# Token-major out projections: 128-token blocks stand still, 512 weight columns move, norms run along the rows

## The chip, the cores and the metric

One core of one Trainium2 chip. The time is device microseconds of one execution of the whole program; a kernel's time is the median of its runs. A profiled execution leaves a trace with every instruction's start, length and what it waited for. Engines are named as in the profile: PE is TensorE's matmuls, PEld its weight loads, DVE is VectorE, ACT ScalarE, POOL GpSimd, SP SyncE, which here issues the DMAs.

## What is computed

One inference step of a trunk with two layers over 640 tokens of 2048 features: 128 context tokens (condition c_ctx) and 512 sample tokens (condition c). In each layer

```
shift, scale, gate = split(silu(cond) @ w_ada + b_ada)
h = rmsnorm(x) * norm_w * (1 + scale) + shift
p = h @ w_in                                   # split among the layer's mixers
x = x + gate * (concat(mixers(p)) @ w_out)     # the out projection, 2048 x 2048
```

The even layer's mixers are a gated DeltaNet and a windowed attention, the odd layer's a gated linear attention and a neighbourhood attention. At the end y = rmsnorm(x) * final_norm_w. The change is in the last line of each layer, in the norm that follows it, and in how x gets from there to layer 1 and to y. Gates differ between the two groups of tokens, not between tokens of a group.

## The kernel before

**Layout.** Activations are feature-major: a slice k of 128 features lies on the partitions, the 640 tokens along the row. Each product is kept near float32 by splitting both factors into a high and a low part of type float32r: three matmuls, high by high, high by low, low by high (`G.mm`, line 77 of the profile, is the call that issues every matmul; `G.tr`, line 84, a transpose).

**Weights.** `weights()` (L1041) brings 256 KB from memory into `w_st` (SyncE's queue, L1046), ScalarE casts it to `w_hi` (L1049) and VectorE subtracts to get `w_lo` (L1051; GpSimd for a few). There are three buffers of each. `Main.load` keeps three such loads ahead of the matmuls, and `Main.step` runs one small group of three matmuls at a time; whoever needs a result calls `until`, which steps until it is there and, every so many steps, advances a side job, the "fill".

**Out projection** (`Outs`, `out_proj` L1503). 16 blocks of 128 output features; the weight block is the stationary operand (128 x 128), 320 tokens move, in two halves, into two accumulators of 128 x 320. The 16 slices of the mixers' output, in an order in which they become ready (ORDER0, ORDER1), are loaded from a buffer in memory and split into `hh` and `hl` by `Outs.stream`. Fourteen blocks are done whole; the last two are done first for tokens 0 to 319, then for 320 to 639, so that the norm of the first half can start early. After a block `residual` loads `x_old` (L1515), computes gate * acc + x_old on VectorE (L1519), writes layer 0's x to memory (L1523), squares it on ScalarE (L1462), sums the squares over blocks on GpSimd (L1463) and multiplies x by the next norm's weight (`scaled`, L1423).

**Norm.** `rstd` sums the squares over the partitions with small matmuls against ones (`n_ss`), takes the root on VectorE (lines 96 to 101), and spreads it to all partitions with another matmul (`n_bc`) and a copy to `n_R`. `times` (L1427) multiplies.

**After the projections.** Layer 0's `end` scales x into `h_t`, adds the shift on ScalarE (`hh`, L1773) and subtracts on VectorE (`hl`, L1774), for each half, and layer 1's first matmuls (`turns`, half by half) start on the first half. Layer 1's `end` scales x and writes yT (L1856).

**The fill of layer 0's projection** is `ada_vec` (L1295): layer 1's shift, computed on VectorE from w_ada, 256 KB a step (`vec`, L1306 the loads, L1318 and L1320 the products), four parts that each end with a few small matmuls (`adv_ps`). It advances once in six groups of three matmuls. From the last two blocks on the order of instructions is pinned to the order of the program (`g.pin`).

Of the kernel before, what the change touches and what calls it, by code (L numbers as in the profile page):

```python
# [18 lines left out]
EPS = 1e-6  # L19
T = 640  # L20
# [43 lines left out]
SMALL = [("bada", 96), ("nw", 32), ("fn", 16), ("convw", 120), ("dtb", 16), ("alog", 16), ("sink", 8), ("onorm_a", 1),  # L64
# [1002 lines left out]
class Main:  # L1067


    def __init__(self, g, hh, hl, part={}, start=0):  # L1070
        self.part, self.start = dict(part), start
        self.g, self.hh, self.hl, self.order = g, dict(enumerate(hh)), dict(enumerate(hl)), range(16)
        self.asked, self.quarters, self.loaded, self.cur, self.n = [], [], [], None, 0
        self.done, self.ready, self.other, self.last = 0, {}, [], []
# [28 lines left out]
    def halves(self, drams):  # L1103

        rs = [[[d, 0, None, False, None, (t,)] for d in drams] for t in range(2)]
        self.last = [(r, q) for t in rs for r in t for q in range(4)]
        return [[self.wait(r, True) for r in t] for t in rs]

    def load(self):
        while len(self.loaded) < LOOK:  # L1110
# [9 lines left out]
            if r[0].shape[1] == 512:  # L1120
# [4 lines left out]
            self.loaded.append((q, work))  # L1125
# [40 lines left out]

    def when(self):
# [6 lines left out]
        q = self.loaded[0][0]  # L1174
        return max(self.ready.get(k, 0 if k in self.hh else INF) for k in self.order[q * 4:q * 4 + 4])
# [72 lines left out]
def ada(g, l, parts, m, store, wait=None):  # L1248
# [26 lines left out]
    for i, (c, d, k0, k1) in enumerate(todo):  # L1275
# [13 lines left out]
        if k1 == 16:  # L1289
            yield LAT["hop"]  # L1290
            ada_out(g, l, parts, c, acc)
            yield


def ada_vec(g, l, part, store, engs, wait=None):  # L1295
# [14 lines left out]
    for i, (c0, k) in enumerate(todo):  # L1310
# [27 lines left out]
        ada_out(g, l, (part,), c0, rows)  # L1338

# [126 lines left out]
class Outs:  # L1466


    def __init__(self, g, main, total, w, order, halves=0):
        self.g, self.main, self.total, self.w, self.order, self.whole = g, main, total, w, order, 16 - halves  # L1470
# [16 lines left out]
    def stream(self):  # L1487
# [4 lines left out]
        self.reqs = [m.ask(self.w[n], n, True) for n in range(self.whole)]  # L1492
        self.halves = m.halves([self.w[n] for n in range(self.whole, 16)])
# [9 lines left out]
def out_proj(g, l, outs, pool, x_old, x_spill, fill, scale, end=None):  # L1503
# [4 lines left out]
    accs, xs, todo, xos = [], [], [], {}  # L1508
    main, reqs = outs.main, outs.reqs
    gate = g.mod[l, 2]  # L1510

    def residual(n, ps):
        if n not in xos:
            xos[n] = g.pt2.tile([128, T], F32, name="x_old", bufs=4)
            nc.sync.dma_start(xos[n], x_old(n))  # L1515
            xs.append(pool.tile([128, T], F32, name=f"x{n}"))
        for t in ps:
            for c0, c1, cd in ((0, 128, 0), (128, 320, 1)) if t == 0 else ((320, 640, 1),):
                nc.vector.scalar_tensor_tensor(out=xs[n][:, c0:c1], in0=ps[t][:, c0 - t * 320:c1 - t * 320],  # L1519
                                               scalar=gate[:, n, cd:cd + 1], in1=xos[n][:, c0:c1], op0=ALU.mult, op1=ALU.add)  # L1520
        cs = slice(min(ps) * 320, max(ps) * 320 + 320)
        if x_spill is not None:
            nc.sync.dma_start(x_spill(n)[:, cs], xs[n][:, cs])  # L1523
        square_sum(g, pool, accs, xs[n], n, nc.gpsimd, cs=cs)
        todo.append((n, cs))
        while todo and scale(todo[0][0]) is not None:
            i, cs = todo.pop(0)
            scaled(g, xs[i], scale(i), cs)

    for n in range(outs.whole):  # L1530
        ps = main.until(reqs[n], fill, 6)
        if n == 15:
            for _ in fill:
                pass
        residual(n, ps)
    g.pin = True
    for t in range(2 if outs.whole < 16 else 0):
        for n in range(outs.whole, 16):
            residual(n, main.until(outs.halves[t][n - outs.whole], fill, 3))
        for _ in fill:  # L1540
            pass
        fill = end(t, xs, accs)
    for _ in fill:
        pass
    return xs, accs


def body(nc, tc, I, O):
    off = [(k, v.shape[1]) for k, v in const_table().items()]
    with ExitStack() as es:  # L1550
        g = G()
        g.nc, g.tc, g.I, g.O = nc, tc, I, O
        g.mod, g.mods = {}, {}
# [25 lines left out]
        g.fn, g.dtb, g.alog, g.sink = (cuts[k] for k in ("fn", "dtb", "alog", "sink"))  # L1579
# [68 lines left out]
        x1 = g.pd1.tile([16, 128, T], F32, name="x1_d")  # L1648


        with ExitStack() as e1:
# [98 lines left out]
            outs = g.outs = Outs(g, main, 53, I["w_out_even"], ORDER0, 2)  # L1750
# [235 lines left out]
```

## Time and profile before

| | before |
|---|---|
| median of 3 runs | 2717.81 us (2716.46 to 2723.16) |
| the profiled execution, its span | 2723.34 us, 2721.5 us |
| mean granted TensorE clock | 0.983 |
| matmuls of one out projection, weight loads | 1536 of 128x320, 72 of 256 KB |
| matmuls between 2698 and 2722 us | 17 |

How to read the profile's rows: a timeline row has the start and length in us, the engine, the line, the operation, the tiles written and read, the shapes, and in brackets the engine's idle time before it and what ended it. "128*128 128x320 f32" is a stationary operand of 128 columns and an output of 128 x 320. A group row has a count, the busy time and the mean length in ns; a mean mixes what the group mixes. In a table of stretches, each engine has its busy time and, in brackets, its number of instructions; the clock is the one granted to TensorE, and the DMA share can come out above 1. Matmuls overlap, so their price is the distance of starts and not the length. SPq rows are DMA issues, with the time that the queue took for the issue and not for the transfer.

### The profile page before, as it was taken

The page shows a single profiled execution, that of the slowest core. Times are in us where ns is not written, and L with a number is a line of the kernel's source. Part 1 is how long each engine was busy: PE and PEld are TensorE (multiplying, and loading weights), DVE is VectorE, ACT ScalarE, POOL GpSimd, SP SyncE. Part 2 cuts the span into 40 slices and gives each one's busy share as a digit, 9 for nine tenths or more (in the row PEclk, how much of TensorE's full clock was granted, in tenths as well). Part 3 has the DMA queues.
Part 4 walks back from the last instruction along what each step waited for, and adds up shares of the span by engine and source line. Part 5 has one row for each costly group of instructions (what it writes and reads, how often), then busy time and mean ns, then how long its engine had stood idle before and what let it go on. Part 6 is the DMA issues. An engine that isn't in the chain of part 4 may idle for free.

```text
span 2721.5 us, 54637 instructions
## 1 busy us (share of the span) xinstructions
PE 2601.2 (96%) x21303; PEld 2435.2 (89%) x21303; DVE 1536.9 (56%) x3598; ACT 954.0 (35%) x2150; POOL 704.9 (26%) x894
## 2 busy tenths in 40 slices
PE   6989999999999999999999899999999999999996
PEld 4779788988978997799998899999999999998996
DVE  5766546656556565357876755546453644545225
ACT  3232343433433343442224443343333434233222
POOL 2326514253251550001223330012001301221113
PEclk9989999999999999999999999999999999999998
DMA  9932434243243424246653413323232222325324
GB/s 334 309 97 71 116 95 122 81 133 116 85 126 111 123 60 136 72 143 200 214 186 115 127 64 105 106 76 97 81 108 90 87 93 87 98 69 183 99 97 136
DMA packets 264706, 329.85 MB, mean 121 GB/s; under 512 B 76013, under 2 KB 148925, under 8 KB 264447
## 3 DMA queue, kind: packets, MB, share of 16 engines
q1 hardware_dynamic: 264447, 326.35, 38.2%
q8 instruction: 168, 2.75, 0.4%
q14 instruction: 91, 0.75, 0.1%
HBM read 294.95 MB, written 28.68 MB: 119 GB/s over the span
## 4 chain that ended last, share of the span: by engine, by line
PE 44%; DVE 3%; DMA 2%; issue 1%; ACT 0%; DVEq 0%; SPq 0%; ACTq 0%
PE acc L77 38%; PE at_s L77 1%; PE at_o L77 1%; DMA vec<-w_ada 1%; PE c_lv L77 1%; DVE hl L1774 1%; DVE vec L1320 1%; PE c_ops L77 1%; PE tm_ps L84 1%; PE c_U L77 0%; DVE x L1427 0%; PE at_pt L84 0%; DVE w_lo L1051 0%; PE c_bp L77 0%; DMA hl<-o_d 0%
## 5 line engine op out<-in xcount | busy, mean ns | idle before, releaser
L77 PE MATMUL acc<-hh,w_hi 128*128 128x320 f32 (+1 forms) x4544 | 1446.7, 319 | 18.7 <-ACT w_hi L1049 5.7
L77 PE MATMUL acc<-hl,w_hi 128*128 128x320 f32 (+1 forms) x4544 | 1415.6, 312 | 7.7 <-DVE hl L1229 7.7
L77 PE MATMUL acc<-hh,w_lo 128*128 128x320 f32 x4480 | 1394.4, 311 | 4.8 <-DVE w_lo L1051 4.8
L77 PEld LDWEIGHTS acc<-hh,w_hi 128*128 128x128 f32 (+1 forms) x4544 | 856.5, 189 | 59.8 <-issue 32.8
L77 PEld LDWEIGHTS acc<-hl,w_hi 128*128 128x128 f32 (+1 forms) x4544 | 857.5, 189 | 12.9 <-DVE hl L1229 11.0
L77 PEld LDWEIGHTS acc<-hh,w_lo 128*128 128x128 f32 x4480 | 847.3, 189 | 7.4 <-DVE w_lo L1051 6.7
L1051 DVE TENSOR_TENSOR w_lo<-w_st,w_hi 128x512 fp32r<-128x512 f32 x561 | 439.1, 784 | 588.1 <-ACT w_hi L1049 578.5
L1049 ACT CAST w_hi<-w_st 128x512 fp32r<-128x512 f32 (+1 forms) x604 | 365.2, 605 | 925.1 <-PE acc L77 783.9
L1320 DVE SCALAR_TENSOR_TENSOR vec<-vec,cond 128x256 f32<-128x256 f32 (+1 forms) x360 | 212.3, 634 | 23.3 <-DMA vec<-w_ada 21.5
L496 POOL TENSOR_TENSOR i_S<-i_S,i_tmp 40x30 f32<-40x30 f32 (+14 forms) x240 | 141.1, 588 | 18.7
L494 POOL TENSOR_TENSOR i_tmp<-i_S 40x30 f32<-40x30 f32 (+14 forms) x240 | 134.2, 559 | 18.0
L1463 POOL TENSOR_TENSOR n_acc<-n_acc,n_sq 128x640 f32<-128x640 f32 (+1 forms) x30 | 45.9, 1530 | 298.2 <-ACT n_sq L1462 298.2
L77 PE MATMUL ada_ps<-adv,cond 128*32 128x128 f32 x2048 | 94.7, 293 | 25.4 <-DMA adv<-w_ada 24.9
L929 POOL TENSOR_TENSOR c_X<-c_b 128x320 f32<-128x320 f32 x56 | 46.1, 822 | 221.9 <-PE c_lv L77 195.0
L77 PEld LDWEIGHTS ada_ps<-adv,cond 128*32 128x32 f32 x2048 | 48.7, 113 | 53.5 <-DVE n_acc L1463 19.4
L215 DVE SCALAR_TENSOR_TENSOR a_y<-a_pad,consts,a_y 128x644 f32<-128x644 f32 x96 | 89.7, 934 | 2.2
L790 POOL TENSOR_TENSOR d_bias<-d_braw,d_mask 128x256 f32<-128x256 f32 x32 | 27.9, 905 | 231.8 <-PE tm_ps L84 90.7
L1287 DVE TENSOR_TENSOR adv<-adv,ada_ps 128x128 f32<-128x128 f32 x144 | 40.5, 281 | 73.3 <-PE ada_ps L77 72.4
L301 POOL TENSOR_TENSOR a_at<-a_df,consts 128x640 f32<-128x640 f32 x8 | 13.7, 1712 | 253.9 <-DVE a_ss L269 222.0
L665 POOL TENSOR_TENSOR b_sw<-b_sw,b_tab 128x512 f32<-128x512 f32 x10 | 14.9, 1491 | 234.8 <-DMA b_sw<-b_q 199.7
L404 ACT ACTIVATE a_ot<-a_st,g_egc 128x128 f32<-128x128 f32 x72 | 26.4, 367 | 107.2 <-PE a_st L77 105.7
L1051 POOL TENSOR_TENSOR w_lo<-w_st,w_hi 128x256 fp32r<-128x256 f32 (+1 forms) x43 | 36.3, 851 | 106.6 <-ACT w_hi L1049 89.0
(310 smaller groups left out, 2760.6 us busy)
## 6 DMA issues: line engine op xcount, KB each, us to landing
adv<-w_ada SPq DMA_DIRECT2D x256, 256.0 KB
w_st<-w_in_odd SPq DMA_DIRECT2D x232, 256.0 KB
w_st<-w_in_even SPq DMA_DIRECT2D x188, 256.0 KB
w_st<-w_out_even SPq DMA_DIRECT2D x72, 256.0 KB
w_st<-w_out_odd SPq DMA_DIRECT2D x72, 256.0 KB
vec<-w_ada SPq DMA_DIRECT2D x64, 256.0 KB
vec<-w_ada SPq DMA_DIRECT2D x128, 128.0 KB
hl<-o_d SPq DMA_DIRECT2D x31, 320.0 KB
```

The lines of the kernel that those rows point to most:

```text
L77: i = self.nc.tensor.matmul(out, lhsT=lhsT, rhs=rhs, **kw)
L84: i = self.nc.tensor.transpose(out, x, ident)
L215: nc.vector.scalar_tensor_tensor(out=y, in0=pad[:, j:j + CL], scalar=w[:, j:j + 1], in1=y, op0=ALU.mult, op1=ALU.add)
L494: E.tensor_tensor(out=t, in0=S[:, j + 1:, j].unsqueeze(2).to_broadcast([40, n, j]), in1=S[:, j, 0:j].unsqueeze(1).to_broadcast([40, n, j]) ...
L496: E.tensor_tensor(out=S[:, j + 1:, 0:j], in0=S[:, j + 1:, 0:j], in1=t, op=ALU.add)
L790: nc.gpsimd.tensor_tensor(out=bias[:, j], in0=braw[:, :, x0:x0 + 32], in1=g.dmask[:, j * 32:j * 32 + 32].unsqueeze(1).to_broadcast([128, 8 ...
L929: nc.gpsimd.tensor_tensor(out=pv(X[0])[:, :, 1 - d], in0=bv[:, :, 1 - d], in1=bm, op=ALU.subtract)
L1049: nc.scalar.copy(hi, st)
L1051: (nc.gpsimd if g.spare >= 0 else nc.vector).tensor_tensor(out=lo, in0=st, in1=hi, op=ALU.subtract)
L1287: nc.vector.tensor_add(acc, acc, ps)
L1320: nc.vector.scalar_tensor_tensor(out=acc[:, c], in0=st, scalar=sc, in1=acc[:, c], op0=ALU.mult, op1=ALU.add)
L1463: eng.tensor_add(accs[0][:, cs], accs[0][:, cs], t[:, cs])
```

## The change

Both out projections are turned round. Their order of loops, the layout of x, the norms and the output change with that; the mixers and the input projections don't.

- **Matmuls.** The stationary operand is a 128 x 128 piece of the mixers' output: slice k, tokens of block b. The moving one is 512 columns of w_out, slice k, laid out so that one load of 256 KB holds one slice (`by_512`; before, a load held four slices of 128 columns). Accumulators are 128 tokens x 512 features, in two pools of three (`pacc`, `pax`); the general pool `psg` goes from four to two. There are four column blocks n and five token blocks b. For n = 0 and n = 3 the tokens go in two groups, (0, 1, 2) and (3, 4), for n = 1 and 2 all five at once: 6 passes over 16 slices, 96 loads a projection, 960 matmuls of 512 columns.
- **Residual.** The gate now varies along the row: `gate_rows` transposes it, stores it to memory once, and `out_proj` loads it spread over all partitions for each n (128 x 2 x 512). VectorE multiplies the accumulator by it into `g_t`, GpSimd adds that to x (VectorE for n = 3), ScalarE squares with a running sum along the row (`n_ss`). x is loaded token-major from a new input and, in layer 1, from the spilled copy; the loads of the next n are asked for when an n begins. Layer 1 multiplies by the final norm's weight, a new input spread over the partitions (1 MB in the tile), on GpSimd for n < 3.
- **Norm.** `token_rstd` sums four numbers per token and takes the root on VectorE; no matmuls.
- **Layer 0's end.** Each token block is scaled by a number per partition (blocks shared out to ScalarE, VectorE and GpSimd), then 80 transposes bring x back to feature-major, ScalarE applies scale and shift, VectorE casts `hh`, GpSimd subtracts `hl`. The first group's stand among the matmuls of the last pass.
- **Layer 1's end.** y is scaled and written token-major, 256 KB a store.
- **The fill** advances once in three groups.

The diff, cut to its core (the first `end` is layer 0's, the second layer 1's):

```diff
+    def wide(self, drams):
+        parts = [(0, 1, 2), (3, 4)]
+        rs = []
+        for n, d in enumerate(drams):
+            for bl in parts if n in (0, len(drams) - 1) else [(0, 1, 2, 3, 4)]:
+                rs.append([d, 0, {}, set(), None, bl, n])
...
+    def tokens(self, r, i, w):
...
+        for b in r[5]:
...
+            cs = slice(b * 128, b * 128 + 128)
+            for x, wt, e in ((self.hh, hi, 0), (self.hh, lo, 1), (self.hl, hi, 2)):
+                g.mm(r[2][b], lhsT=x[k][:, cs], rhs=wt, start=i == 0 and e == 0, stop=i == 15 and e == 2)
...
-def out_proj(g, l, outs, pool, x_old, x_spill, fill, scale, end=None):
+def out_proj(g, l, outs, pool, x_old, x_spill, fill, every, end, fn=None):
...
+    def load(n):
+        if n < 4:
+            cs = slice(n * 512, n * 512 + 512)
+            gates[n] = g.pt2.tile([128, 2, 512], F32, name="gate", bufs=2)
+            nc.sync.dma_start(gates[n], g.gate[l][:, cs].unsqueeze(0).to_broadcast([128, 2, 512]))
+            for b in range(5):
+                nc.sync.dma_start(xs[b][:, cs], x_old(b)[:, cs])
...
+        for b in bl:
+            ps = main.until(main.block(r, b), fill, every)
+            x = xs[b][:, cs]
+            t = g.pt2.tile([128, 512], F32, name="g_t", bufs=2)
+            nc.vector.tensor_tensor(out=t, in0=ps, in1=gates[n][:, int(b > 0)], op=ALU.mult)
+            (nc.vector if n == 3 else nc.gpsimd).tensor_tensor(out=x, in0=x, in1=t, op=ALU.add)
+            if x_spill is not None:
+                nc.sync.dma_start(x_spill(b)[:, cs], x)
+            junk = g.pt2.tile([128, 512], F32, name="n_sq")
+            nc.scalar.activation(junk, x, AF.Square, accum_out=ss[:, b, n:n + 1])
+            if fn is not None and n < 3:
+                nc.gpsimd.tensor_tensor(out=x, in0=x, in1=fn[:, cs], op=ALU.mult)
...
+            def end(bl, xs, ss):
+                yield
+                r = token_rstd(g, px, ss, bl)
...
+                for k in range(16):
+                    ps = g.psg.tile([128, 3, 128], F32, name="h_ps", tag="gen")
+                    for j, b in enumerate(bl):
...
+                        g.tr(ps[:, j], x, g.c["ident"])
...
+            def end(bl, xs, ss):
+                r = token_rstd(g, px, ss, bl)
...
+                for n in (3, 0, 1, 2):
...
+                        nc.sync.dma_start(O["y"][b][:, cs], x)
```

SyncE's queue where layer 1's projection begins, before (`hl` is the last slice of the mixers' output, `x_old` a block of x, `w_st` the weights):

```order
L1499 DMA hl_28634<-o_d 128x640
L1515 DMA x_old<-x_d 128x640
L1046 DMA w_st<-w_out_odd 128x512
L1515 DMA x_old<-x_d 128x640 x3
L1046 DMA w_st<-w_out_odd 128x512
```

and after (`fn` the final norm's weight, `x_28291` to `x_28295` the five token blocks):

```order
L1536 DMA hl_28251<-o_d 128x640
L1931 DMA fn<-fn 128x2048
L1585 DMA gate<-gate_d_28189 128x2x512
L1587 DMA x_28291<-x_d 128x512
...
L1587 DMA x_28295<-x_d 128x512
L1585 DMA gate<-gate_d_28189 128x2x512
L1587 DMA x_28291<-x_d 128x512
...
L1587 DMA x_28295<-x_d 128x512
L1046 DMA w_st<-w_out_odd 128x512 x3
```

Seven slices of weights have been asked for by then; the eighth to tenth (k7 to k9) now follow fn, two gates and ten x, where one x_old stood before. The same queue where layer 0's projection begins, before:

```order
L1046 DMA w_st<-w_out_even 128x512
L1306 DMA vec<-w_ada 128x512 x4
L814 DMA d_mask<-d_tab 128x256
L781 DMA d_v<-cn_v 128x128
L1046 DMA w_st<-w_out_even 128x512
```

and after:

```order
L1046 DMA w_st<-w_out_even 128x512
L1587 DMA x_15320<-x 128x512
...
L1587 DMA x_15324<-x 128x512
L1341 DMA vec<-w_ada 128x512 x4
L1046 DMA w_st<-w_out_even 128x512 x3
L1587 DMA x_15320<-x 128x512
```

Ten loads of x now stand with the four of vec ahead of the seventh slice (k6), and behind the three slices k6 to k8 come ten more with three of vec. VectorE in the first blocks of layer 0's projection, before (`vec` is the fill):

```order
L1320 SCALAR_TENSOR_TENSOR vec<-vec,cond 128x512 x4
L1051 TENSOR_TENSOR w_lo<-w_st,w_hi 128x512
L1320 SCALAR_TENSOR_TENSOR vec<-vec,cond 128x512 x4
L1051 TENSOR_TENSOR w_lo<-w_st,w_hi 128x512
L1320 SCALAR_TENSOR_TENSOR vec<-vec,cond 128x512
```

and after, in the second group of n = 0:

```order
L1355 SCALAR_TENSOR_TENSOR vec<-vec,cond 128x512 x2
L1051 TENSOR_TENSOR w_lo<-w_st,w_hi 128x512
L1355 SCALAR_TENSOR_TENSOR vec<-vec,cond 128x512
L1051 TENSOR_TENSOR w_lo<-w_st,w_hi 128x512
L1355 SCALAR_TENSOR_TENSOR vec<-vec,cond 128x512 x2
L1051 TENSOR_TENSOR w_lo<-w_st,w_hi 128x512
```

A weight difference now stands behind one or two steps of the fill instead of four.

More of the change, by code (lines that the diff above doesn't have):

```diff
@@ L1101, in turns, with block @@
         return [both(r) for r in rs]
[L1103 to L1107, printed above, removed]
+    def wide(self, drams):
[4 more added lines that the diff above has]
+                rs.append([d, 0, {}, set(), None, bl, n])
+        self.last = [(r, i) for r in rs for i in range(16)]
+        return rs
+    def block(self, r, b):
+        while b not in r[3]:
+            yield lambda: b in r[3]
+        return r[2][b]
     def load(self):
@@ L1119, in load @@
             r, q = self.quarters.pop(0)
[L1120 removed]
+            ks = range(q * 4, q * 4 + 4)
+            if r[0].shape[1] == 8192:
+                work = self.tokens(r, q, weights(self.g, r[0], q * 4, q * 4 + 4))
+                ks = [q]
+            elif r[0].shape[1] == 512:
                 work = self.narrow(r, q, narrow(self.g, r[0], q))
@@ L1338, in ada_vec @@
         ada_out(g, l, (part,), c0, rows)
+        if part == 2 and c0 + width == 2048:
+            yield 5
+            gate_rows(g, l)
 def ada_put(g, l, part, n0, ps):
@@ L1500, in stream, with gate_rows @@
                 self.take(k, x, lo)
-def out_proj(g, l, outs, pool, x_old, x_spill, fill, scale, end=None):
+def gate_rows(g, l):
+    nc = g.nc
+    m = g.mod[l, 2]
+    ps = g.psg.tile([16, 2, 128], F32, name="gr_ps", tag="gen")
+    for c in range(2):
+        g.tr(ps[:, c], m[:, :, c], g.c["ident"])
+    rows = g.pk.tile([16, 2, 128], F32, name="gr", tag="gr")
+    nc.scalar.copy(rows, ps)
+    g.gate[l] = g.pd1.tile([2, 2048], F32, name=f"gate_d{l}")
+    nc.sync.dma_start(g.gate[l].rearrange("c (n p) -> n c p", p=128), rows)
@@ L1506, in out_proj @@
+def out_proj(g, l, outs, pool, x_old, x_spill, fill, every, end, fn=None):
     fill = iter(fill)
     nc = g.nc
[L1508 to L1528, printed above, removed]
@@ L1530, in out_proj @@
-    for n in range(outs.whole):
-        ps = main.until(reqs[n], fill, 6)
-        if n == 15:
+    main = outs.main
+    xs = [pool.tile([128, 2048], F32, name=f"x{b}") for b in range(5)]
+    ss = pool.tile([128, 5, 4], F32, name="n_ss")
+    gates = {}
+    def load(n):
[5 more added lines that the diff above has]
+                nc.sync.dma_start(xs[b][:, cs], x_old(b)[:, cs])
@@ L1533, in out_proj @@
             for _ in fill:
                 pass
[L1535 to L1542, printed above, removed]
+            fill, every = end(bl, xs, ss), 1
     for _ in fill:
         pass
-    return xs, accs
 def body(nc, tc, I, O):
@@ L1552, in body @@
         g.nc, g.tc, g.I, g.O = nc, tc, I, O
-        g.mod, g.mods = {}, {}
+        g.mod, g.mods, g.gate = {}, {}, {}
+        g.pax = None
         g.spare = 0
```

145 lines of the change are left out of this document (96 added, 49 removed).

## The prediction

> **What bounds the kernel now.** I read the page first: the span, the engines' busy shares and the chain that ended last.
>
> ```profile
> span 2721.5 us, 54637 instructions
> PE 2601.2 (96%) x21303; PEld 2435.2 (89%) x21303; DVE 1536.9 (56%) x3598; ACT 954.0 (35%) x2150; POOL 704.9 (26%) x894
> ...
> PE acc L77 38%; PE at_s L77 1%; PE at_o L77 1%; DMA vec<-w_ada 1%; PE c_lv L77 1%; DVE hl L1774 1%; DVE vec L1320 1%; PE c_ops L77 1%; PE tm_ps L84 1%; PE c_U L77 0%; DVE x L1427 0%; PE at_pt L84 0%; DVE w_lo L1051 0%; PE c_bp L77 0%; DMA hl<-o_d 0%
> ```
>
> TensorE is the bound, and the accumulating matmuls are by far the largest piece of the chain. A change to the out projections is worth what it takes from TensorE's time there, plus what it adds or removes at their ends. So I next read a table of stretches: one in the DMA-heavy start of the kernel, two inside layer 0's out projection and the way to layer 1, three around layer 1's, and the tail (columns: window; its length; busy us and instructions of each engine; clock; DMA share; GB/s).
>
> ```profile
> 60.00:80.00 20.00, 18.40 (x258) 16.29 (x249) 13.72 (x30) 3.36 (x8) 5.85 (x7) 1.00 1.07 343
> 1240.00:1300.00 60.00, 60.00 (x423) 59.61 (x422) 49.00 (x77) 13.48 (x21) 12.21 (x11) 1.00 0.69 219
> 1470.00:1525.00 55.00, 44.02 (x274) 39.64 (x273) 45.16 (x99) 29.57 (x71) 23.87 (x21) 0.94 0.34 103
> 2464.00:2480.00 16.00, 14.88 (x101) 13.81 (x99) 13.06 (x23) 8.86 (x15) 0.00 (x0) 1.00 0.90 315
> 2530.00:2590.00 60.00, 60.00 (x411) 60.00 (x410) 16.95 (x29) 13.84 (x22) 12.45 (x13) 1.00 0.30 98
> 2698.00:2722.00 24.00, 2.91 (x17) 1.80 (x15) 14.53 (x29) 0.90 (x2) 12.33 (x13) 0.55 0.56 192
> ```
>
> Inside both projections TensorE is busy without a gap, while VectorE is already at 49 of 60 us in layer 0 and DMA at 0.69. Between the layers 11 us of 55 are idle, and the tail of 24 us has almost no matmul. Those two places can be gained; the steady part can only change with the price of a matmul.
>
> **The change part by part.** *The matmuls.* Their price is the spacing of starts, since the durations overlap. Timeline of TensorE, warm, then the half-clock stretch between the layers:
>
> ```profile
> 1259.69 0.31 PE L77 MATMUL acc<-hh,w_hi 128*128 128x320 f32 x1
> ...
> 1261.16 0.31 PE L77 MATMUL acc<-hl,w_hi 128*128 128x320 f32 x1
> ```
>
> ```profile
> 1511.07 0.47 PE L77 MATMUL acc<-hh,w_hi 128*128 128x320 f32 x1
> ...
> 1515.87 0.42 PE L77 MATMUL acc<-hl,w_hi 128*64 128x320 f32 x1
> ```
>
> Ten warm starts take 1.47 us, 0.1467 each: 320 columns at 2.4 per ns would be 133.3 ns, so 13.3 ns are extra. Eighteen half-clock starts take 4.80 us, 266.7 ns each, which is 320/1.2 with nothing extra. Before, a projection is 16 blocks x 16 slices x 2 halves x 3 = 1536 matmuls, 225.3 us. After, it is 4 x 5 x 16 x 3 = 960 of 512 columns. No row shows 512 columns of this kind. If the extra is fixed for each matmul, one costs 213.3 + 13.3 = 226.7 ns and a projection 217.6 us (-7.7). If it grows with the columns (x1.1), one costs 234.7 ns and a projection 225.3 us (0). If there is none, 213.3 ns and 204.8 us (-20.5). I take the fixed one: an extra that is gone at half clock looks like a step between two matmuls that slower columns hide.
>
> The Trainium skill ("TensorE: Matmul & The Clock Gate", section Back-to-back issue gap) gives N/2.4 + 2.5 ns warm and N/1.2 cold. The cold half agrees with the 266.7 ns here; the warm half would be 135.8 ns for 320 columns, and 146.7 was measured, so the trace decides against it for these operands. By it a matmul of 512 would be 215.8 ns and a projection 207.2 us.
>
> *What feeds them.* Weights, a third more loads (96 of 256 KB instead of 72), casts and differences; the residual, now two passes; the scaling:
>
> ```profile
> L1320 DVE SCALAR_TENSOR_TENSOR vec<-vec,cond 128x512 f32<-128x512 f32 x120 | 97.6, 854 | 1.6 <-DMA vec<-w_ada 1.2
> L1051 DVE TENSOR_TENSOR w_lo<-w_st,w_hi 128x512 fp32r<-128x512 f32 x561 | 439.1, 784 | 588.1 <-ACT w_hi L1049 578.5 <-DMA a_Zt<-inv_out 3.9 <-DMA inv_in<-a_M 2.5
> L1519 DVE SCALAR_TENSOR_TENSOR x<-acc,mod,x_old 128x320 f32<-128x320 f32 x32 | 17.5, 548 | 20.9 <-PE acc L77 20.7
> L1049 ACT CAST w_hi<-w_st 128x512 fp32r<-128x512 f32 x564 | 349.0, 619 | 842.5 <-PE acc L77 751.9 <-issue 42.7 <-DMA w_st<-w_in_even 20.8
> L1423 POOL TENSOR_TENSOR x<-x,mod 128x512 f32<-128x512 f32 x14 | 18.1, 1295 | 0.0
> ```
>
> Twenty-four more casts (15 us on ScalarE) and differences (19 us on VectorE) for each projection are covered by TensorE as long as VectorE isn't full. In n = 0 of layer 0 it is: the second group, blocks 3 and 4, wants a new slice every 6 matmuls (1.36 us), and the order puts one or two vec operations before each difference. About 20 vec, 13 w_lo, three gate multiplications (estimate 0.75 us from the 320-column row) and the copies come to 25 us against 21.8 us of matmuls: +4 (0 to 8). In n = 1 about 44 vec, 17 w_lo and 5 multiplications are at most 55 us against 54.4: just covered. Squares on ScalarE and sums on GpSimd (1.3 us for each of the 15 blocks before n = 3) have five matmul groups of 10.9 us to hide in. The gate rows (two transposes, a copy, a small store) lie earlier, beside other work: 0, at most 1.
>
> *What stands in front of the weights on SyncE's queue.* This is the largest term. SyncE before, at the start of layer 0's projection; then layer 1's, with the projection's first matmul (1536 back from the last) ahead:
>
> ```profile
> 1237.19 1.76 SPq L1306 DMA_DIRECT2D vec<-w_ada  x4
> 1239.05 0.38 SPq L814 DMA_DIRECT2D d_mask<-d_tab  x1
> 1239.47 0.43 SPq L781 DMA_DIRECT2D d_v<-cn_v  x1
> 1241.33 0.33 SPq L1046 DMA_DIRECT2D w_st<-w_out_even  x1
> ```
>
> ```profile
> 2464.89 0.31 PE L77 MATMUL acc<-hh,w_hi 128*128 128x320 f32 x1
> ```
>
> ```profile
> 2477.41 0.32 SPq L1499 DMA_DIRECT2D hl<-o_d  x1
> 2477.83 0.37 SPq L1515 DMA_DIRECT2D x_old<-x_d  x1
> 2478.30 0.38 SPq L1046 DMA_DIRECT2D w_st<-w_out_odd  x1
> ```
>
> Layer 1: the order has fn (1 MB), a gate, five x, a gate and five x between that hl and the seventh weight slice: 1.05 + 2 x 0.52 + 10 x 0.26 = 4.7 MB. At the 343 GB/s of the busiest stretch (60 to 80) that is 13.7 us; the queue is already at 315 GB/s here. So slice k7 lands at about 2491.5, is ready after cast and difference (1.4 us) at 2493. TensorE, which starts at 2464.89 and takes 9 matmuls (2.04 us) for a slice, wants it at 2479: 13.5 us of waiting. k10 stands behind three slices and ten more x (3.4 MB, 10 us) while k7 to k9 last 6.1 us: 3 more. After such a gap the clock is halved for a while (18 matmuls in the rows above, 120 ns each, 2 us). Together +18.5, bounds 0 (the loads go sooner) and 25. Layer 0 has the same in smaller form: ten x and four vec before k6 (3.7 MB, from 1237.2 to 1248) where TensorE, running from 1231.84 with some cold matmuls, wants k6 near 1246; thirteen more loads before k9. I take 2 + 5 and 2 for the clock, +9 (0 to 14).
>
> *Layer 0's end.* Forty-eight of the 80 transposes lie inside the projection. Three such transposes start at 1231.54, the next matmul at 1231.84:
>
> ```profile
> 1231.54 0.55 PE L84 MATMUL at_pt<-consts,at_S 128*128 128x128 f32 x3 [0.21 <-DVE at_S L603]
> 1231.84 0.39 PE L77 MATMUL acc<-hh,w_hi 128*128 128x320 f32 x1
> ```
>
> At 0.1 to 0.11 us: +5.2, and +3 (0 to 6) for h tiles that three buffers and GpSimd's difference (about 1 us a slice) release late. The first half's sums and broadcast on TensorE go: -2.7, priced by the tail's n_ss (1.23) and n_bc (1.43) below. Layer 0 in sum: -7.7 + 4 + 9 + 5.2 + 3 - 2.7 = +10.8.
>
> *Between the layers.* Of the 55 us, 256 matmuls are 37.6; the other 17 are n_ss and n_bc, idle time and half clock. After: 37.6, 32 transposes (3.5), and a norm without matmuls behind 76 matmuls of layer 1 that stand first (11.1 us, against about 6 us of norm and 2.4 of scaling). I leave 4 us of waiting for the last ten pairs of transposes in a row. 45 instead of 54: -9 (-13 to -3).
>
> *Layer 1 in the middle and at its end.* -7.7 - 2.7 + 18.5, +1.5 for n = 0's second group, and +3.5 (0 to 8) because twelve y stores wait on SyncE, each for its scaling, ahead of the last three weight slices. Sum +13.1.
>
> *The tail.*
>
> ```profile
> 2697.27 0.31 PE L77 MATMUL acc<-hh,w_lo 128*128 128x320 f32 x1
> ...
> 2700.17 0.54 DVE L1519 SCALAR_TENSOR_TENSOR x<-acc,mod,x_old 128x320 f32<-128x320 f32 x1
> ...
> 2701.26 1.14 PEld L77 LDWEIGHTS n_ss<-consts,n_acc 128*64 128x64 f32 x10 [3.09 <-ACT n_acc L1459]
> 2701.26 1.23 PE L77 MATMUL n_ss<-consts,n_acc 128*64 128x1 f32 x10 [3.01 <-ACT n_acc L1459]
> ...
> 2702.91 0.53 DVE L96 TENSOR_SCALAR n_r_y<-n_ms 64x5 int32<-64x5 int32 x1
> ...
> 2706.31 0.16 DVE L101 SCALAR_TENSOR_TENSOR n_r_y<-n_r_t,n_r_y 64x5 f32<-64x5 f32 x1
> ...
> 2707.04 1.43 PE L77 MATMUL n_bc<-n_dg,consts 64*128 64x320 f32 x2 [4.55 <-DVE n_dg L1397]
> ...
> 2709.04 7.82 DVE L1427 TENSOR_TENSOR x<-x,n_R 128x320 f32<-128x320 f32 x11 [2.06 <-ACT n_R L1405]
> ```
>
> From the last matmul it is 23.9 us to the end: 2.6 until VectorE is free of the first half's scaling, the sum, 3.5 for the root, the broadcast, 7.8 of scaling, 4.6 of stores. After: product and sum 1.3, square 0.6, reduction 0.4, root 2.5 to 3.5, then eight blocks on two engines (2.4 us) and 256 KB stores (4 to 5). About 13.5: -10.4 (-13 to -7).
>
> *The sum.* +10.8 - 9 + 13.1 - 10.4 = +4.5. The profiled execution took 2723.34 us (its span and 1.8 around it), 5.5 above the median of three, 2717.81; added to the median, 2722 us.
>
> **The rivals.** A measurement here tells about 0.3% (8.2 us) from no change: 2709.7 to 2726.0.
>
> A, slower: the extra grows with the columns. Each 512 takes 234.7 ns, nothing is won on the matmuls, and 2 x 7.7 comes on top from the first group on: 2737 us. For it: the exact factor 1.100. Against it: nothing but the vanishing at half clock, which a limit on reading the moving columns would explain as well. Chance 0.20.
>
> B, faster: the warm price is that of a plain stream, 213.3 to 216 ns; 2 x 960 x 11 to 13 ns are 21 to 26 us: 2699 us. Against it: 320 columns cost 10.8 ns more than such a stream would. Chance 0.10. The Trainium skill's section named above gives this price.
>
> C, faster: the first loads don't delay the weights, since x and fn are sent before TensorE is in the projection or the queue keeps up. Then 27.5 us go: 2695 us. Against it: SyncE issues in order and the share is 0.90 where they are added. Chance 0.14.
>
> D, slower: VectorE, at 49 of 60 us, stays full through n = 0 and n = 1 of layer 0: +10, 2732 us. Against it: GpSimd has less to do there, and vec is faster alone. Chance 0.06.
>
> **How the numbers follow.** The forecast (0.50), with the unknown terms at half their bounds, spans 2711 to 2734: 0.03 of it faster, 0.32 same, 0.15 slower. A adds 0.18 slower and 0.02 same, B 0.09 faster and 0.01 same, C 0.13 and 0.01, D 0.05 slower and 0.01 same: faster 0.25, same 0.37, slower 0.38. The range 2698 to 2741 cuts off the outer halves of A and of C with B.
>
> **What would show it.** Starts of 512-column matmuls 226 to 227 ns apart; TensorE idle for 10 us or more near the seventh slice of layer 1 and some 5 us in layer 0, with a half clock behind it; a stretch between the layers near 45 us; a tail near 13.5. I am wrong if the spacing is another one (A, B), or if TensorE is busy throughout the first 40 us of both projections (C).

## The result, and the profile after

The changed kernel takes 2746.05 us (median of 4 runs, 2739.04 to 2750.0) against 2718.12 us (4 runs) of the kernel before: a ratio of 1.0097, 95% interval [1.0072, 1.0122], 27.9 us slower. The forecast was 2722 us with a range of 2698 to 2741. The profiled execution took 2750.0 us, the longest of the four.

The page of the changed kernel: the span, the engines and the chain.

```profile
span 2748.2 us, 52533 instructions
PE 2602.9 (95%) x20147; PEld 2348.1 (85%) x20147; DVE 1548.2 (56%) x3569; ACT 998.5 (36%) x2258; POOL 672.2 (24%) x842
...
PE acc L77 56%; PE a_st L77 3%; DMA adv<-w_ada 2%; PE ada_ps L77 2%; PE at_o L77 2%; PE at_s L77 2%; DVE w_lo L1051 1%; POOL i_S L496 1%; POOL i_tmp L494 1%; DMA vec<-w_ada 1%; PE at_pt L84 1%; PE c_ops L77 1%; DMA x<-x_d 1%; DMA w_st<-w_out_even 1%; PE c_lv L77 1%
```

TensorE still bounds the program, but weight loads and loads of x now stand in the chain with it. The stages, each from the start of its first matmul to the start of its last, show where the time went:

| stage | before, us | after, us | difference | forecast |
|---|---|---|---|---|
| layer 0's projection | 239.0 | 263.9 | +24.9 | +10.8 |
| from there to layer 1's projection | 994.0 | 987.1 | -6.9 | -9 |
| layer 1's projection | 232.4 | 250.4 | +18.0 | +13.1 |
| tail | 24.2 | 14.8 | -9.4 | -10.4 |

The tail runs from the last matmul's start to the end of the span. The price of a 512-column matmul, from TensorE's timeline in the middle of layer 0's projection:

```profile
1344.68 0.39 PE L77 MATMUL acc<-w_hi,hh 128*128 128x512 f32 x1
...
1347.18 0.39 PE L77 MATMUL acc<-w_hi,hl 128*128 128x512 f32 x1
```

Eleven spacings in 2.50 us are 227 ns each; the median spacing over both projections is 227 ns. That is 213.3 + 13.3, the fixed extra. 960 of them are 217.6 us, so the matmuls did give back 7.7 us a projection. So what was lost was lost around them: in TensorE's waits, in the matmuls at half clock behind these waits, and in the 48 transposes of layer 0's last pass (5.2 us). By pass, from a table of stretches (first group of n = 0, second group, second group of n = 3 in layer 0; first group of n = 0 and second group of n = 3 in layer 1; the same matmuls without a gap would take 32.6, 21.8, 21.5, 32.6 and 21.5 us):

```profile
1231.95:1281.85 49.90, 40.70 (x154) 31.70 (x153) 34.83 (x53) 13.17 (x24) 0.25 (x1) 0.86 0.85 288
1281.85:1311.68 29.83, 26.28 (x115) 19.18 (x113) 24.78 (x40) 11.28 (x21) 4.65 (x3) 0.94 0.73 235
1456.94:1495.84 38.90, 32.23 (x145) 23.53 (x144) 31.58 (x54) 27.50 (x58) 24.77 (x19) 0.91 0.37 111
2482.93:2536.16 53.23, 38.78 (x157) 30.22 (x156) 21.79 (x35) 17.64 (x30) 0.00 (x0) 0.84 0.81 283
2700.76:2733.36 32.60, 25.79 (x96) 19.88 (x95) 17.67 (x40) 14.02 (x26) 0.00 (x0) 0.90 0.60 194
```

In between, n = 1 and n = 2 take 54.4 us each in layer 1, which is 240 matmuls without a gap, and 56.1 and 56.5 in layer 0. So it is the passes with two groups of tokens that lose: 17 (with some attention matmuls that stood there before as well), 8 and 17 us (5 of them the transposes') in layer 0, 21 and 11 in layer 1.

Three places show it best. SyncE where layer 1's projection begins, and TensorE behind it:

```profile
2495.86 0.37 SPq L1931 DMA_DIRECT2D fn<-fn  x1
2496.32 0.38 SPq L1585 DMA_DIRECT2D gate<-gate_d  x1
2496.76 3.26 SPq L1587 DMA_DIRECT2D x<-x_d  x5
2500.06 1.43 SPq L1585 DMA_DIRECT2D gate<-gate_d  x1
2501.53 6.17 SPq L1587 DMA_DIRECT2D x<-x_d  x5
2508.11 2.36 SPq L1046 DMA_DIRECT2D w_st<-w_out_odd  x3
```

```profile
2514.97 1.65 PE L77 MATMUL acc<-w_hi,hh 128*128 128x512 f32 x3 [11.68 <-ACT w_hi L1049]
```

The weights are issued 12 us behind fn, and TensorE waits 11.7 us for their cast; the bracket names the cast, but ScalarE had itself waited for the load. SyncE and ScalarE at layer 1's end:

```profile
2713.42 8.21 SPq L1945 DMA_DIRECT2D y<-x  x12
2721.72 1.78 SPq L1046 DMA_DIRECT2D w_st<-w_out_odd  x3
```

```profile
2726.76 1.94 ACT L1049 CAST w_hi<-w_st 128x512 fp32r<-128x512 f32 x3 [8.62 <-DMA w_st<-w_out_odd]
```

Twelve stores of y, 3 MB, pass ahead of the last three weight slices. TensorE at the first transposes of layer 0's end:

```profile
1464.94 0.39 PE L77 MATMUL acc<-w_hi,hl 128*128 128x512 f32 x1
1468.67 0.69 PE L84 MATMUL h_ps<-consts,x 128*128 128x128 f32 x2 [3.34 <-ACT x L1566]
```

They need the norm of the first group of tokens and its first scaling, and TensorE runs out of matmuls 3.3 us before these are there. Some of the matmuls behind this wait then run at half clock (0.43 us from start to start). VectorE and GpSimd in the same pass:

```profile
1467.90 1.71 DVE L1568 TENSOR_SCALAR x<-x,n_r_y 128x512 f32<-128x512 f32 x3
```

```profile
1468.03 5.38 POOL L1568 TENSOR_SCALAR x<-x,n_r_y 128x512 f32<-128x512 f32 x3 [37.83 <-issue]
...
1484.88 2.42 POOL L1857 TENSOR_TENSOR hl<-h_t,hh 128x384 fp32r<-128x384 f32 x2 [0.36 <-PE h_ps L84]
```

A scaling takes GpSimd 1.79 us (VectorE's take 0.57) and a subtraction 1.21 us, against about 1.0 us for the three matmuls and three transposes that TensorE does for each slice of h. The tail, last, is what was expected (VectorE, then SyncE):

```profile
2733.11 1.37 DVE L1601 TENSOR_TENSOR g_t<-acc,gate 128x512 f32<-128x512 f32 x2 [3.69 <-PE acc L77]
...
2739.20 1.41 DVE L1942 SCALAR_TENSOR_TENSOR x<-x,n_r_y,fn 128x512 f32<-128x512 f32 x2
```

```profile
2739.94 4.47 SPq L1945 DMA_DIRECT2D y<-x  x8
```

### The profile page after: what moved, and what is told of

It is laid out like the page before. It is cut to its first block, busy times and chain, and to the rows that moved or that the text cites. A ratio compares the mean times of both kernels' runs of the same rounds, so it can differ in the third digit from the quotient of the medians.

```text
span 2748.2 us, 52533 instructions
## 1 busy us (share of the span) xinstructions
PE 2602.9 (95%) x20147; PEld 2348.1 (85%) x20147; DVE 1548.2 (56%) x3569; ACT 998.5 (36%) x2258; POOL 672.2 (24%) x842
## 4 chain that ended last, share of the span: by engine, by line
PE 71%; DMA 9%; issue 7%; DVE 6%; POOL 4%; ACT 2%; SPq 1%; ACTq 0%; DVEq 0%; POOLq 0%
PE acc L77 56%; PE a_st L77 3%; DMA adv<-w_ada 2%; PE ada_ps L77 2%; PE at_o L77 2%; PE at_s L77 2%; DVE w_lo L1051 1%; POOL i_S L496 1%; POOL i_tmp L494 1%; DMA vec<-w_ada 1%; PE at_pt L84 1%; PE c_ops L77 1%; DMA x<-x_d 1%; DMA w_st<-w_out_even 1%; PE c_lv L77 1%
## 5 line engine op out<-in xcount | busy, mean ns | idle before, releaser
L77 PE MATMUL acc<-hh,w_hi 128*128 128x320 f32 (+1 forms) x3520 | 1129.7, 321 | 7.5 <-ACT b_vT L640 2.6
L77 PE MATMUL acc<-hl,w_hi 128*128 128x320 f32 (+1 forms) x3520 | 1097.0, 312 | 7.9 <-DVE hl L1261 7.7
L77 PE MATMUL acc<-hh,w_lo 128*128 128x320 f32 x3456 | 1076.4, 312 | 2.0 <-DVE w_lo L1051 2.0
L77 PEld LDWEIGHTS acc<-hh,w_hi 128*128 128x128 f32 (+1 forms) x3520 | 663.1, 188 | 45.0 <-issue 28.1
L77 PEld LDWEIGHTS acc<-hl,w_hi 128*128 128x128 f32 (+1 forms) x3520 | 662.8, 188 | 12.5 <-DVE hl L1261 11.0
L77 PEld LDWEIGHTS acc<-hh,w_lo 128*128 128x128 f32 x3456 | 652.8, 189 | 4.2 <-DVE w_lo L1051 3.2
L77 PE MATMUL acc<-w_hi,hh 128*128 128x512 f32 x640 | 250.0, 406 | 27.9 <-ACT w_hi L1049 26.3
L77 PE MATMUL acc<-w_lo,hh 128*128 128x512 f32 x640 | 257.5, 402 | 5.0 <-DVE w_lo L1051 4.8
L77 PE MATMUL acc<-w_hi,hl 128*128 128x512 f32 x640 | 254.7, 398 | 0.0
L77 PEld LDWEIGHTS acc<-w_lo,hh 128*128 128x128 f32 x640 | 124.1, 194 | 36.6 <-DVE w_lo L1051 11.9
```

The lines of the kernel that those rows point to most:

```text
L77: i = self.nc.tensor.matmul(out, lhsT=lhsT, rhs=rhs, **kw)
```

## The experiments

The theory after the result, "order": the waits come from what stands ahead of the weights, in SyncE's queue above all, and from VectorE and GpSimd at two places; they are separate and can each be taken away. The rival, "feed": the passes with two groups can't be fed at all by 256 KB for 6 or 9 matmuls. Later a third came in, "look-ahead": three loads ahead are too few. Every run is compared with the kernel before on the same chip, where that kernel's median lay between 2713.97 and 2719.21 us. The last three columns are stages of the one profiled execution of each run.

A difference between two rows of medians is uncertain by 7 to 10 us where one of them is the change. The stages are steadier for a single edit: the stretch ahead of layer 0's projection, which e1 to e9 leave as it was, took from 1221 to 1232 us in the profiles of the change and of these runs.

| run | us | ratio to before, 95% | above before, us | layer 0 | between | layer 1 |
|---|---|---|---|---|---|---|
| the kernel before | | 1 | 0 | 239.0 | 994.0 | 232.4 |
| the change | 2746.05 | 1.0097 [1.0072, 1.0122] | +27.9 | 263.9 | 987.1 | 250.4 |
| e1 x staged | 2729.72 | 1.0054 [1.0037, 1.0071] | +15.8 | 253.1 | 986.5 | 247.2 |
| e2 y stores late | 2742.24 | 1.0100 [1.0076, 1.0124] | +28.3 | 261.9 | 986.2 | 250.2 |
| e3 less on GpSimd | 2737.39 | 1.0081 [1.0060, 1.0102] | +23.4 | 257.5 | 985.6 | 250.1 |
| e4 fill from n = 1 | 2751.22 | 1.0126 [1.0100, 1.0152] | +37.3 | 268.0 | 987.8 | 249.5 |
| e5 y stores held | 2741.77 | 1.0087 [1.0060, 1.0114] | +24.7 | 261.1 | 985.7 | 244.2 |
| e6 no fill | 2730.84 | 1.0051 [1.0035, 1.0067] | +13.8 | 247.2 | 986.7 | 249.7 |
| e7 other queue | 2743.93 | 1.0086 [1.0061, 1.0112] | +26.9 | 263.8 | 986.7 | 244.5 |
| e8 all ordered by hand | 2744.98 | 1.0089 [1.0065, 1.0113] | +27.9 | 267.6 | 997.5 | 233.0 |
| e9 four mends | 2717.33 | 0.9990 [0.9980, 1.0000] | -1.9 | 250.2 | 981.7 | 241.5 |
| e10 four mends, four buffers | 2701.60 | 0.9931 [0.9912, 0.9950] | -17.6 | 241.4 | 982.8 | 230.6 |
| e11 four buffers alone | 2734.84 | 1.0056 [1.0037, 1.0075] | +15.6 | 261.2 | 983.1 | 242.3 |
| e12 before, no fill | 2714.75 | 0.9984 [0.9971, 0.9998] | -4.5 | 229.9 | 990.2 | 233.5 |
| e13 before, four buffers | 2718.70 | 0.9994 [0.9977, 1.0010] | -0.1 | 240.3 | 983.4 | 236.5 |

**e1, x staged.**

```diff
-            for b in range(5):
-                nc.sync.dma_start(xs[b][:, cs], x_old(b)[:, cs])
+            xin[n, b] = g.pt2.tile([128, 512], F32, name="x_in", bufs=5)
+            nc.sync.dma_start(xin[n, b], x_old(b)[:, cs])      # for n + 1 behind the sum of (n, b)
```

> The changed kernel with x read through five rotating staging buffers of 128x512, so that a block's x for the next n is asked for only when the block's sum has freed a buffer; the same bytes are loaded, but 5 x loads instead of 20 can stand ahead of the first weights of each projection. Theory 'order' (the weights wait because x, gate and fn stand ahead of them in SyncE's queue): in layer 0 the stalls of 3.3 us at slice k6 and 4.0 at k9, and most of the half-clock matmuls behind them (3 to 4 us), go; in layer 1 3.4 MB instead of 4.7 MB stand ahead of k7, and its stall shrinks from 11.8 to about 8 us. Together -12 us, 2734 us. Theory 'feed' (the first passes starve on the weights' own denser loads and on the fill, whatever x does): no more than 2 us gained, 2744 to 2746 us.

Measured: 12.2 us gained, as "order" had it (10.8 and 3.2 in the two projections). Layer 0's first pass falls from 49.9 to 37.8 us, and layer 1's first pass from 53.2 to 49.0; the wait at the eighth slice of layer 1 is 7.3 us. SyncE there, with TensorE behind it:

```profile
2470.91 0.37 SPq L1940 DMA_DIRECT2D fn<-fn  x1
2471.38 0.38 SPq L1585 DMA_DIRECT2D gate<-gate_d  x1
2471.81 3.38 SPq L1593 DMA_DIRECT2D x_in<-x_d  x5
2475.23 1.15 SPq L1585 DMA_DIRECT2D gate<-gate_d  x1
2477.78 10.49 SPq L1046 DMA_DIRECT2D w_st<-w_out_odd  x4
```

```profile
2487.25 1.22 PE L77 MATMUL acc<-w_hi,hh 128*128 128x512 f32 x2 [7.28 <-ACT w_hi L1049]
```

**e7, other queue.** The same loads issued by GpSimd:

```diff
-                nc.sync.dma_start(xs[b][:, cs], x_old(b)[:, cs])
+                nc.gpsimd.dma_start(xs[b][:, cs], x_old(b)[:, cs])      # the gate rows and fn too
```

> The changed kernel with the loads of x, the gate rows and fn issued by GpSimd on its own queue instead of SyncE's; the same bytes at the same time. Theory 'order in the queue': the weights no longer stand behind them, the 11.8 us stall at k7 of layer 1 falls below 4 us and the two of layer 0 (3.5 and 2.7) below 2 together: -12 to -16 us, 12 to 16 us above before. Rival 'bandwidth' (5 MB more must be moved at that point, whichever queue they are in): the stalls change place but stay within 4 us in sum, 24 to 28 us above before.

Measured: 1 us in all, by the median. By stages the two layers differ. In layer 1 the wait of 11.7 us at the eighth slice is gone, with no wait for a cast above 0.9 us from 2480 to 2530; the first pass fell from 53.2 to 44.6, the next one is 2.6 longer, and the projection fell by 6 to 244.5. Layer 0's projection kept its length, 263.8 us, with a wait for a cast of up to 5.7 us. In its first stretch the DMA engines are full (a stretch of the table, then the DMA view's row for those loads, us from issue to landing last):

```profile
1240.00:1250.00 10.00, 5.00 (x19) 3.03 (x17) 4.67 (x7) 0.62 (x1) 5.58 (x11) 1.00 1.04 386
```

```profile
x<-x POOLq DMA_DIRECT2D x20, 256.0 KB, 6.8
```

Neither theory holds alone: order in the queue made the long wait of layer 1, and in layer 0, where 5 MB are asked for at once, the weights were as late from another queue. The Trainium skill ("DMA: Bandwidth & Descriptors", section Issuing engines are not separate DMA queues) states that DMAs run on the same 16 DMA engines whichever engine starts them. The share of 1.04 at 386 GB/s, with x issued by GpSimd and the weights by SyncE, agrees. So e1 probably worked in layer 0 because it asked for less at that time, and not only because the order changed.

**e2 and e5, the y stores.** e2 issues the first group's stores at the end of the generator; e5 also fixes SyncE's order there.

```diff
-                        nc.sync.dma_start(O["y"][b][:, cs], x)
+                            late.append((O["y"][b][:, cs], x))
...
+                for y, x in late:
+                    held(g, nc.sync.dma_start(y, x))      # e5; in e2 without held()
```

> The changed kernel with the first group's twelve y stores of layer 1's end issued after the last weight slices instead of as soon as each block is scaled. Theory 'order': the stall of 4.6 us ahead of the last three slices and its half clock (2 us) go, the 2.1 us one (casts behind ScalarE's scaling) stays; -6 to -7 us, less up to 1 us in the tail where the stores now end: 2739 to 2741 us. Rival (the weights' casts wait for ScalarE and VectorE, which scale at that point, and the stores only fill the gap): 2745 us.

> The changed kernel with the twelve y stores of layer 1's first group held, by a fixed program order on SyncE, behind the last weight slice (in the run with late stores nine of the twelve still stood ahead of it). The changed kernel stands 27.9 us above the kernel before. Theory 'order': the stall of 4.6 us ahead of the last three slices and its half clock go, the last pass of layer 1 takes 25 to 27 us instead of 32.6; 21 to 22 us above before. Rival (ScalarE's scaling ahead of the casts): the last pass stays above 31 us and the kernel 27 to 28 us above before.

e2 gained nothing: the scheduler, which orders whatever is not pinned to the program's order, put nine of the twelve stores ahead of the last three weight slices all the same, so it tested little. e5 did what was meant (the last pass of layer 1):

```profile
2697.69:2722.38 24.69, 22.40 (x96) 17.49 (x95) 17.60 (x40) 13.93 (x26) 0.00 (x0) 1.00 0.61 192
```

24.7 us instead of 32.6, where "order" had 25 to 27. The projection is 6.2 us shorter; the medians' 3.2 us are within their noise. The wait of 2.1 us ahead of the eleventh slice stayed, and the tail stayed at 14.8.

**e3, less on GpSimd.**

```diff
-                        per_token(g, ("act", "dve", "pool")[j], x if n < 3 else xl[b], x, r[:, j:j + 1])
+                        per_token(g, ("act", "dve", "dve")[j], x if n < 3 else xl[b], x, r[:, j:j + 1])
-                    nc.gpsimd.tensor_tensor(out=lo, in0=h, in1=hi, op=ALU.subtract)
+                    (nc.gpsimd if k % 2 else nc.vector).tensor_tensor(out=lo, in0=h, in1=hi, op=ALU.subtract)
```

> The changed kernel with layer 0's end taken off GpSimd in part: its third of the scaling goes to VectorE, and every other low-part subtraction too. Theory 'GpSimd paces' (1.2 us for a subtraction and 1.8 us for a scaling against 1.0 us of TensorE work for a slice): between the end of the last pass and the first group's transposes the time falls from 22.7 to about 17 us, -5 us, 2741 us. Rival (ScalarE and VectorE, which also do casts there, are as full): within 2 us of 2746.

Measured: 4.5 us by the medians, near the expected 5 but within their noise. The last pass of layer 0 falls from 38.9 to 35.5, and that is what can be put down to GpSimd; TensorE's wait for the first scaling stayed (4.2 us here).

**e4, e6 and e12, the fill.**

```diff
-            ps = main.until(main.block(r, b), fill, every)
+            ps = main.until(main.block(r, b), fill if n else None, every)      # e4
...
-                     ada_vec(g, 1, 0, vec_store(px, 4, 2), ("dve", "dve")), 3, end)
+                     (), 3, end)      # e6; the same in the kernel before for e12
```

> The changed kernel with the fill of layer 0's projection started at n = 1 instead of at n = 0 (three of its 72 steps are then left for the end of the first group of n = 3). Theory 'VectorE and the fill crowd n = 0': the stalls of the second group of n = 0 (6.6 us) go, and k6 has no vec loads ahead (-1 MB, about -2 us); -7 us, 2739 us. Theory 'order' alone: -2 us for the missing vec loads, 2744 us. A loss of some 2 us is possible at n = 3 where the rest of the fill is run at once.

> The changed kernel without the fill of layer 0's projection: layer 1's shift is left out (zeros), with its 64 loads, 128 VectorE operations and four small groups of matmuls. Theory 'the fill crowds layer 0': the second group of n = 0 falls from 29.8 to about 22.7 us (what it takes in layer 1, where there is no fill), n = 1 and n = 2 from 56.3 to 54.4 each, n = 0's first group by 3 to 5 us, as 1 MB less stands ahead of k6: together -14 to -17 us, 11 to 14 us above before. Rival (three weight buffers can't bring a slice in 1.36 us anyway, fill or not): the second group stays near 28 us and the gain is 4 to 6 us, from the small matmuls and n = 1 and 2.

> The kernel before without the fill of layer 0's projection (layer 1's shift is left out, zeros). In the changed kernel leaving it out is worth 14 us. Theory 'lost cover' (before, the fill is hidden, and the change made it cost): only its 72 small matmuls and the short waits beside them go, -4 to -6 us. Rival (the fill costs as much in the kernel before, so the change did nothing to it): -12 to -15 us.

Without the fill, in e6 and e12, the kernel leaves out layer 1's shift.

e4 lost 9 us by the medians, about as much as their noise, and 4 in layer 0's projection, where a gain was expected, a miss: the order of VectorE is not fixed in n = 0, and the fill was pulled forward into it anyway, while its rest piled up at the end. VectorE in n = 0, and the stretch before layer 0's last pass:

```profile
1273.35 1.41 DVE L1355 SCALAR_TENSOR_TENSOR vec<-vec,cond 128x512 f32<-128x512 f32 x2
```

```profile
1423.00:1464.00 41.00, 35.81 (x181) 28.05 (x179) 39.24 (x61) 14.90 (x31) 5.59 (x4) 0.96 0.71 226
```

e6 settles it: without the fill 14.1 us go by the medians, 16.7 in layer 0's projection. The first two passes of layer 0:

```profile
1228.35:1272.08 43.73, 38.17 (x154) 29.89 (x151) 15.51 (x23) 12.75 (x22) 0.25 (x1) 0.92 0.67 224
1272.08:1295.47 23.39, 22.91 (x98) 17.61 (x96) 12.27 (x18) 11.31 (x22) 4.70 (x3) 1.00 0.67 198
```

29.8 become 23.4 and 49.9 become 43.7. In the kernel before the same fill costs 4.5 us by the medians (e12, interval 0.5 to 7.9) and 9.1 in layer 0's projection: without it seven of the sixteen blocks are 1 us shorter and the first one 2. So the fill was not quite hidden before either, and by the stages some 8 us of the loss is cover that the old projection gave it and the new one doesn't.

**e8 and e9, the mends together.** e8 has e1's staging, e3, e5, gate and fn in pieces, and all loads of weights, x, gate and fn in program order on SyncE; e9 has the same mends with only layer 1's end ordered.

```diff
+            fn[n] = g.pt2.tile([128, 512], F32, name="fn", bufs=2)
+            nc.sync.dma_start(fn[n], g.I["fn"][:, cs].to_broadcast([128, 512]))      # e8 and e9
...
+        if pend:                             # e8: gate, fn and one x between weight slices
+            pend.pop(0)()
```

> The changed kernel with all of it put right as far as the order goes: x in staging buffers, gate and fn in 512-column pieces, each asked for between weight slices and in fixed order on SyncE; less on GpSimd at layer 0's end; y stores behind the last weights. By the theory 'order' the parts add up: -12 (x staged), -6 (the rest of the stall at k7 of layer 1, 7.4 us there), -4.5 (GpSimd), -6 (stores): 28 us, level with before, -3 to +4. Rival (each stall that goes uncovers the next one, the three-deep look-ahead): 8 to 14 us above before.

> The changed kernel with four mends and the scheduler left free elsewhere: x in five staging buffers (alone -12.2 us), less on GpSimd at layer 0's end (alone -4.5), y stores held behind the last weights (alone -3.3, -6 by its stage), gate and fn in pieces of 512 columns (0.5 MB less ahead of k7, -1.5). If the stalls are separate, as theory 'order' has it, they add up: 27.9 - 21 to 24 = 4 to 7 us above before. Rival (a stall that goes uncovers the next): 10 to 14 us above before.

e8 came out level with the change, a miss. Layer 1's projection did come down to 233.0 us, but layer 0's rose to 267.6 and the way between them by 10. In layer 0, in fixed order, the weights stand behind the stores of x, which wait for GpSimd's sums; layer 1 has no such stores. Why the way grew was not looked into. SyncE's waits in layer 0's projection, e8 and then the change (us in total, times, longest):

```profile
SPq L1630 <- POOL x L1626: 27.6, 14, 8.2
```

```profile
SPq L1604 <- POOL x L1602: 10.0, 12, 1.0
```

e9, with the scheduler free elsewhere, took off all 29.8 us, more than either theory had. The two projections are 22.6 us shorter in sum; e1's two, e3's last pass and e5's layer 1 make 23.6 by themselves. So in the projections the mends add up, and that the stalls only uncover one another is not what happened. The other 7 us (5.4 of them between the projections, in the profile) were not traced to a mend.

**e10, e11 and e13, look-ahead.**

```diff
-LOOK = 3
+LOOK = 4
...
-    st = g.pw.tile([128, 4, 128], F32, name="w_st", tag="w_st", bufs=3)[:, 0:n]
+    st = g.pw.tile([128, 4, 128], F32, name="w_st", tag="w_st", bufs=4)[:, 0:n]      # w_hi and w_lo too
```

> The same four mends with four weight buffers of each kind and a look-ahead of four loads instead of three. Theory 'look-ahead' (a load covers only 9 or 6 matmuls of 512 columns, 2.0 or 1.4 us, in the passes with two groups, where it covered 24 of 320, 3.5 us, before; so three loads ahead cover 4 to 6 us instead of 10): one more load takes 1.4 to 2 us off every stall of those passes, 6 to 9 us in all; level with before, -3 to +1. Rival (VectorE is full there, depth changes nothing): within 2 us of the mended kernel with three.

> The changed kernel with nothing but the fourth weight buffer and load ahead. Theory 'look-ahead': the stalls at k6, k9, k7 of layer 1 and the last three slices each lose 1.4 to 2 us and the crowded second group of n = 0 some 4 us; -8 to -12 us, 16 to 20 us above before. Rival (the stalls are set by how many bytes and how much VectorE work stand ahead, not by depth): 26 to 28 us above before.

> The kernel before with the fourth weight buffer and load ahead, and nothing else. Theory 'look-ahead': in its projections a load covers 24 matmuls of 320 columns (3.5 us), so three ahead cover 10 us and a fourth finds nothing to hide there: the two projections stay within 2 us of 239 and 233 us; a gain can come only from the rest of the program, where the changed kernel gained about 4 us between the projections: 0 to -6 us. Rival (the fourth buffer is worth to any version what it was worth to the changed one, mended -15.6 and alone -12.3): -10 us or more, and then the mended deep kernel doesn't beat the old layout at equal depth by more than 5 us.

One more load ahead is worth 12.3 us to the change, 15.7 to the mended kernel (about twice what was expected), and nothing to the kernel before as a whole (0.9994, [0.9977, 1.0010]). There the way between the projections became 10.6 us shorter, but the projections did not (240.3 and 236.5), while e10's are 8.8 and 10.9 us shorter than e9's. The second group of n = 0 in layer 0 and the last pass of layer 1, with four mends and then with four buffers as well:

```profile
1263.63:1293.80 30.17, 25.76 (x116) 17.99 (x114) 26.55 (x40) 11.77 (x22) 4.65 (x3) 1.00 0.78 254
...
2671.24:2697.26 26.02, 23.75 (x97) 18.89 (x95) 17.64 (x40) 13.93 (x26) 0.00 (x0) 0.93 0.62 200
```

```profile
1271.83:1296.36 24.53, 23.91 (x116) 18.17 (x114) 23.81 (x36) 11.30 (x21) 4.67 (x3) 1.00 0.86 289
1442.11:1475.31 33.20, 29.85 (x144) 22.94 (x143) 30.86 (x67) 26.52 (x58) 7.63 (x8) 0.95 0.42 129
...
2666.85:2688.68 21.83, 21.83 (x97) 17.68 (x95) 16.80 (x39) 13.23 (x25) 0.00 (x0) 1.00 0.62 198
```

The last pass of layer 1 now runs without a gap, which answers "feed" there; layer 1's projection takes 230.6 us, less than before, and layer 0's 241.4. In e11, without the mends, the second group of n = 0 did not gain: it took 33.6 us with 25 of the fill's products in it, where the change had 18. e10 beats both kernels: 17.6 us below before, 45.5 below the change by the same comparison. But its two projections together only come level with those before (472.0 and 471.4 us): the profile's gain lies in the tail (14.9 us) and in the way between them, and e13 has that way as short (983.4). In layer 0's last pass (33.2 us against 26.7 for its matmuls and transposes) TensorE still waits 3.1 us for the first scaling behind the norm; VectorE has 30.9 us there. Whether either can be mended was not tried.

## Why the prediction was wrong

Most mechanisms were those of the forecast. The sizes in the passes with two groups were not, and one wait was not in the sum.

- *The price of 512 columns.* Right: 227 ns, the fixed extra, and -7.7 us a projection. Rivals A (234.7) and B (213 to 216) both fall. The Trainium skill's warm price ("TensorE: Matmul & The Clock Gate", section Back-to-back issue gap) gives an estimate of 215.8 ns; the measured spacing decides against it for these operands, at 512 columns as at 320.
- *The loads ahead of the weights.* Right in place and kind: 11.7 us at the eighth slice of layer 1, its first pass 20.6 us over its matmuls (forecast +18.5), 12 us taken off layer 0's first pass and 4 off layer 1's by staging x. SyncE's order was only a part of the cause in layer 0, as e7 shows. Rival C falls.
- *The way to layer 1 and the tail.* Right: -6.9 and -9.4 against -9 and -10.4.
- *The step that failed* is the pricing of the waits at the ends of the projections and in n = 0's second group. "+3 (0 to 6) for h tiles that three buffers and GpSimd's difference (about 1 us a slice) release late" came to 12 (38.9 us less 21.5 of matmuls and 5.2 of transposes). The wait of 3.3 us for the first group's norm and first scaling, with half clock behind it, is in that figure and stands nowhere in the sum; GpSimd's 1.79 us a scaling and its differences gave back 3.4 (e3). "+3.5 (0 to 8) because twelve y stores wait on SyncE" came to 11, 8 of them the stores' (e5). "+4 (0 to 8)" in n = 0's second group came to 8. Together these are some 20 us more than forecast, most of the 23 between 4.5 and 27.9.
- *VectorE in n = 0.* The prediction's list for the second group (20 vec, 13 w_lo, three multiplications) comes to 29.5 us by the means of its own rows, not 25; lengths overlap, and the pass had 24.8 us of VectorE in 29.8. So the 25 was about right and VectorE was not full, yet TensorE waited for its weights. Rival D, VectorE full through n = 0 and n = 1, named one of the places, but n = 1 took only 56.1 us, 1.7 over its matmuls. The fill cost 17 us in layer 0's projection, 8 more than before (e6, e12).
- *Why two of them failed together.* The waits were priced one by one, by the work or the bytes that stand ahead. A load now covers 6 or 9 matmuls (1.4 or 2.0 us) instead of 24 (3.5 us), and e10 against e9, and e13, show that with three loads ahead this thin cover makes small delays into waits in n = 0's second group and in layer 1's last pass. It takes a delay as well: in the last two blocks of the kernel before a load covered 12 matmuls (1.8 us), and TensorE did not wait for weights there. Layer 0's last pass gained only 1.9 us by the fourth buffer (35.1 to 33.2), so its failure is for the larger part another one. That the range was too narrow because these terms move together is argued from this, not measured.

## What to carry to other kernels

When a change lets a load feed fewer matmuls, work out the look-ahead in microseconds, not in buffers: a delay of more than that becomes TensorE waiting, and one more buffer may be worth more than the change, as here. A prefetch with nothing to wait for was pulled to the front of its queue here, where it took the weights' place and their bandwidth; a rotating buffer ties it to the time when it is wanted. A fixed order on a queue is worth it only where nothing in that order waits for a slow engine. And whatever stands between two groups of matmuls, such as a norm, needs its own term in the sum.

## What the runs showed of the hardware

- A matmul of high and low parts costs 13.3 ns beyond its columns at 2.4 per ns, at 320 columns (146.7 ns) as at 512 (227 ns), and nothing beyond them in the half-clock rows (266.7 ns at 320, which is 1.2 per ns).
- GpSimd's scaling of 128x512 took 1.79 us where VectorE's took 0.57.
- Moving 5 MB of loads to another issuing engine's queue left layer 0's projection at 263.8 us, against 263.9, with a DMA share of 1.04; layer 1's fell from 250.4 to 244.5.
